# Attention over 32 sequences of mixed length: running counts in place of token waits, early zero rows, stores on two queues, a tiled first batch and branch hints

## The chip, the cores and the metric

The kernel runs on one core of a Trainium2 chip. The metric is the device time of one execution in microseconds (us). Three runs of the kernel before took 423.67, 424.69 and 424.82; their median is 424.69.

## The reference

There are 32 sequences of at most 512 rows, 8 heads of 64 columns, and a length for each sequence (64 to 511). Rows beyond a sequence's length are zero in the output.

```
output = np.zeros_like(x)                      # (32, 512, 512) float32
for b in range(batch):
    seq_len = lengths[b]
    qkv = np.matmul(x[b, :seq_len], w_qkv)     # w_qkv: (512, 1536)
    q, k, v = np.split(qkv, 3, axis=-1)        # then (8 heads, seq_len, 64)
    scores = scale * np.matmul(q, k.transpose(0, 2, 1))
    attn = np.exp(scores - scores_max)
    attn = attn / (np.sum(attn, axis=-1, keepdims=True) + 1e-08)
    output[b, :seq_len] = np.matmul(attn, v).transpose(1, 0, 2).reshape(seq_len, dim)
```

The lengths are known to the kernel only when it runs; the draw is the same each time.

## The kernel before

**Order of the batches.** On the chip the 32 lengths are sorted in falling order, and the batches are taken in 16 pairs. Each pair gets a class N, the longer length rounded up to a multiple of 32, and T, the number of 128-row tiles in N. For this draw the classes are 512 and 448 (T=4), 384, 352 three times, 320 and 288 (T=3), 256, 224 twice, 192 and 160 twice (T=2), and 128 and 96 (T=1). Classes 480 and 416 do not occur. Every engine's program holds one loop body per class that a pair can have, one behind the other (`loops`, L571): a compare and branch enters body k, a second one at its end goes back to its start, and the program falls through or jumps over a body whose class has no pair. At each body's start `next_class` (L562) loads the following pair's class from a table.

**A body.** It has two halves, h = 0 and 1. Half h does the attention of batch h of the pair: scores (tokens S of the order, into the PSUM buffers s0 and s1 in turn), their exp on ACT, then attention times values (A0 to A3, two heads each), which DVE normalizes by a reciprocal (L370), a mask (L376 or L385) and a multiplication (L396) into `onat`. In the same half stand the projections of the other batch of the sorted order, g = 1 − h: for T ≥ 3 Q and K of two heads each, for T=2 both in one group of two (B0 to B3), and values V0 to V3; these go to the PSUM banks a0 and a1 in turn and are emptied by DVE (L275, L308). `ORDER` (L420) is the order of these tokens, written out by hand for T=4, 3 and 2; T=1 has its own in `half` (L426).

**Waits.** Each instruction that needs another engine's result is preceded by `take` (L34): a wait until a semaphore has reached a number and an instruction that takes the number off again, line 37 in the profile. Only then does the engine go on.

**Queues.** SP issues the transposes of x into xT (L621, one for each 128 rows, from the float16 copy that POOL casts, L768), the loads of x (L629), and for each half two stores of 256 columns each (L675; for T=1 one store, L683). Each store waits for the half's normalization (`s_of`). The order in a half is: transposes, for T=3 a fill of zero rows (L594), store 0, load, store 1. For T=2 and T=1 ACT issues the fills of zero rows at the body's start.

**The first batch.** Lengths are sorted; meanwhile the weights arrive. x of the first batch comes as two loads of 512 KB (L638). DVE casts half of the query and key weights (L866) and then x (L870), ACT the other half (L715). TensorE transposes x in 16 steps (L519) into `pa`, ACT and DVE empty one bank each (L530, L532), and the projections of the first batch follow. POOL writes the start value 0.01 of the exp buffer `ep` (L761).

Of the kernel before, what the change touches and what calls it, by code (L numbers as in the profile page):

```python
# [21 lines left out]
class Prog:  # L22


    def __init__(self, busy, pair=None):
        self.ops = {"pe": [], "act": [], "dve": []}
        self.busy = dict(busy)
        self.pair = {"s0": pair, "s1": pair}
        self.signals = []
# [4 lines left out]
    def take(self, eng, sem, n=1):  # L34
        def fn(e):
            e.wait_ge(sem, n)
            e.nop().then_inc(sem, -n)  # L37

        self.ops[eng].append(fn)
# [35 lines left out]
def kernel(  # L75
# [32 lines left out]
    zt = sb("zt", [P, D], FP32)  # L108
    len_b = sb("len_b", [B, 2 * B], I32)
# [25 lines left out]
    pa16 = pa.bitcast(F16)  # L135
    pav = nc.alloc_psum_tensor("pav", [P, 2 * MAXS], FP32).ap()
# [9 lines left out]
    s_x0 = [sem("s_x00"), sem("s_x01")]  # L146
    s_c0 = [sem("s_c00"), sem("s_c01")]
# [3 lines left out]
    s_zero = sem("s_zero")  # L151
    s_zd = sem("s_zd")
# [3 lines left out]
    s_wr = {g: sem(f"s_wr{g}") for g in ("act", "dve", "v")}  # L156
# [16 lines left out]
    free = {b: sem(f"e_{b}") for b in banks}  # L173
# [7 lines left out]
    def group(pr, b, eng, mms, evac):  # L181
        if b in free:
            acquire(pr, b)
# [10 lines left out]
        pr.add("pe", pe)  # L194
        pr.take(eng, full[(b, eng)])
# [120 lines left out]
    def attnv(pr, h, i, T):  # L316
# [35 lines left out]
        else:  # L352
# [15 lines left out]
        group(  # L368
            pr, "av", "dve", mms,
            lambda e: e.reciprocal(out=rv, in_=den).then_inc(s_r, 1),  # L370
        )
        pr.take("dve", s_r)
        if h == 0 or T == 1:
            pr.add(
                "dve",
                lambda e: e.tensor_scalar(  # L376
                    out=last, in0=last, scalar1=3.0e38, scalar2=now[0][:, 1, T - 1 : T],
                    op0=ALU.min, op1=ALU.mult,
                ).then_inc(s_m, 1),
            )  # L380
        else:
            byt = flat.rearrange("p (t a) -> p t a", t=T)
            pr.add(
                "dve",
                lambda e: e.scalar_tensor_tensor(  # L385
                    out=byt, in0=byt, scalar=3.0e38,
                    in1=now[0][:, 1, 0:T].unsqueeze(2).broadcast_to(list(byt.shape)),
                    op0=ALU.min, op1=ALU.mult,
                ).then_inc(s_m, 1),
            )  # L390
        for j in (0, 1) if T == 1 else (i // 2,) if T != 4 or i % 2 == 0 else ():
            pr.take("dve", s_od[h][j], 16)
        pr.take("dve", s_m)

        def mult(e):
            ins = e.tensor_tensor(  # L396
                out=dst,
                in0=num,
                in1=rv.unsqueeze(len(sh) + 1).broadcast_to([P, *sh, HD]),
                op=ALU.mult,  # L400
            )
            if fin:
                ins.then_inc(s_of[h][i // 2], 1)

        pr.add("dve", mult)

    def acquire_carry(pr, mms):
# [16 lines left out]
    }  # L424

    def half(pr, h, T, N, st):  # L426
# [10 lines left out]
        if T == 1:  # L437
            start_proj()
            qk(pr, st["bank"], g, [(i, 0) for i in range(NPAIR)], N, P)
            qk(pr, st["bank"] ^ 1, g, [(i, 1) for i in range(NPAIR)], N, P)  # L440
            vproj(pr, st["bank"], g, 0, 1)
            pr.signals.append(s_xtf[g])
            pr.take("pe", s_on[h])
            attnv(pr, h, 0, 1)
            acquire(pr, f"a{st['bank'] ^ 1}")
            scores(pr, h, g, 0, 0, 1, N)
            st["bank"] ^= 1
# [3 lines left out]
        first = True  # L451
        for tok in ORDER[T].split():
            if tok == "S":
                i, k = units.pop(0)
                scores(pr, st["slot"], g if i == 0 else h, i, k, T, N)
                st["slot"] ^= 1
            elif tok[0] == "A":
# [3 lines left out]
                attnv(pr, h, int(tok[1]), T)  # L461
            else:
                start_proj()
                i = int(tok[1])
                if tok[0] == "V":
                    vproj(pr, st["bank"], g, i, T)
                elif tok[0] == "B":
                    qk(pr, st["bank"], g, [(i, 0), (i, 1)], N, 256)
                else:
                    qk(pr, st["bank"], g, [(i, "QK".index(tok[0]))], N, MAXS)  # L470
                st["bank"] ^= 1
        assert not units

    def make_body(N):
        T = -(-N // P)
        pr = Prog(CANON, 0)
        for g in ("pe", "act", "dve"):
            pr.add(g, lambda e: next_class(e))
        st = {"slot": 0, "bank": 0}
        for h in range(2):  # L480
            st["x"] = False
            pr.add("dve", lambda e: set_now(e))
            half(pr, h, T, N, st)
# [25 lines left out]
    def make_prologue():  # L509
        pr = Prog({})  # L510
        pr.add("pe", lambda e: e.wait_ge(s_id, 1))

        def tr(e):
            for j in range(2):
                e.wait_ge(s_c0[j], 1)
                for t in (2 * j, 2 * j + 1):
                    for c in range(NC):
                        o = pa16[:, c // 2, (c % 2) * MAXS + t * P : (c % 2) * MAXS + (t + 1) * P]
# [396 lines left out]
```

## Time and profile before

| what | us |
|---|---|
| median of three runs | 424.69 |
| the profiled execution | 426.59 |
| its span in the profile | 424.8 |
| start, up to the first projection | 17.9 |
| first batch's projections | 17.1 |
| bodies with T=4 (2 pairs) | 83.5 |
| bodies with T=3 (6 pairs) | 164.5 |
| bodies with T=2 (6 pairs) | 103.4 |
| bodies with T=1 (2 pairs) | 31.5 |
| last multiplication to the end | 6.9 |

The stages are stretches of the one profiled execution, from a first matmul to the next stage's first. PE is TensorE's matmuls, PEld its weight loads, DVE VectorE, ACT ScalarE, POOL GpSimd, SP the engine that issues most DMAs; a row with a "q" behind the engine (SPq, ACTq, PEq) is that engine's queue or sequencer. A timeline row gives start, length, engine, line, operation, output from input, the count of like instructions, and in brackets the idle time before it with what ended it. A row of the waits gives engine, tile and line, what was waited for, the sum in us, how often, and the longest.

### The profile page before, as it was taken

To read this page: it belongs to the slowest core of one execution; us is meant where nothing else is said; L and a number is where in the kernel's file an instruction comes from. 1 tells how busy PE (TensorE), PEld (TensorE's weight loads), DVE (VectorE), ACT (ScalarE), POOL (GpSimd) and SP (SyncE) were. 2 spreads that over 40 slices of the span, in tenths; PEclk is the share of its full clock that TensorE was granted. 3 is DMA by queue.
4 is the path that set the end of the run, shared out by engine and by line. 5 is a ranking of instruction groups with operands and counts; after the bars stand their busy time and mean duration, and the time that the engine had idled before them with its cause. 6 is when DMAs were issued, how large, how long until landed. Compare 5 with 4: busy or idle time off the path is not lost. (4 is left out here: it accounts for less than half of the span.)

```text
span 424.8 us, 13689 instructions
## 1 busy us (share of the span) xinstructions
PE 354.6 (83%) x4818; PEld 255.4 (60%) x4819; DVE 252.8 (60%) x539; ACT 208.4 (49%) x270; POOL 66.8 (16%) x91
## 2 busy tenths in 40 slices
PE   0589999799889999999999999998788888785741
PEld 0237666466546666666666666677677777674530
DVE  4546666366626666666666756667666676665331
ACT  3035778477636666665666645545334342331000
POOL 5912020202011011100111001111112111210100
PEclk9999999899969999999999999999999999999676
DMA  7854454446535545556455564694676757767471
GB/s 281 313 161 139 150 103 151 96 151 94 177 89 158 168 132 169 167 158 200 125 164 181 158 192 111 185 275 138 221 203 198 260 138 240 250 164 254 83 257 53
DMA packets 83019, 73.35 MB, mean 173 GB/s; under 512 B 42512, under 2 KB 62992, under 8 KB 82960
## 3 DMA queue, kind: packets, MB, share of 16 engines
q1 hardware_dynamic: 77472, 61.04, 50.0%
q10 hardware_dynamic: 5488, 11.54, 7.4%
q8 instruction: 35, 0.57, 0.6%
q14 instruction: 24, 0.20, 0.2%
HBM read 29.37 MB, written 33.55 MB: 148 GB/s over the span
## 5 line engine op out<-in xcount | busy, mean ns | idle before, releaser
L245 ACT ACTIVATE ep<-psc 128x704 f16<-128x704 f32 (+5 forms) x265 | 204.0, 820 | 195.0 <-ACTq L37 195.0
L203 PE MATMUL pa<-xT,w_r 128*128 128x352 f16 (+11 forms) x1056 | 166.7, 296 | 32.8 <-PEq L37 32.3
L275 DVE CAST qkT<-pa 128x352 f16<-128x352 f32 (+5 forms) x192 | 108.0, 563 | 96.5 <-DVEq L37 95.3
L203 PEld LDWEIGHTS pa<-xT,w_r 128*128 128x128 f16 x1056 | 84.4, 101 | 85.2 <-issue 67.1
L203 PE MATMUL pa<-w_r,xT 128*128 128x128 f16 (+1 forms) x1296 | 96.8, 223 | 1.6 <-PEq L37 1.1
L203 PEld LDWEIGHTS pa<-w_r,xT 128*128 128x128 f16 x1296 | 79.2, 98 | 16.7 <-issue 10.3
L203 PE MATMUL psc<-qkT 64*128 64x352 f16 (+11 forms) x656 | 71.6, 303 | 12.0 <-PEq L37 11.9
L308 DVE TENSOR_TENSOR v_aug<-pa,masks 128x384 f16<-128x384 f32 (+2 forms) x116 | 60.8, 524 | 27.1 <-DVEq L37 25.3
L203 PEld LDWEIGHTS pav<-v_aug,ep 128*128 128x128 f16 x1792 | 70.1, 98 | 10.3 <-issue 2.2
L203 PE MATMUL pav<-v_aug,ep 128*128 128x65 f16 x1792 | 74.8, 195 | 0.2 <-issue 0.2
L773 POOL CAST v_aug<-masks 128x24 f16 (+4 forms) x33 | 9.1, 274 | 334.9 <-POOLq L586 334.9
L396 DVE TENSOR_TENSOR onat<-pav,rcp 128x512 f32<-128x512 f32 (+1 forms) x68 | 53.4, 785 | 10.0
L203 PEld LDWEIGHTS psc<-qkT 64*128 64x128 f16 x656 | 25.9, 94 | 33.2 <-issue 22.9
L768 POOL CAST x<-x_nat 128x1536 f16<-128x1536 f32 (+3 forms) x34 | 43.9, 1291 | 5.2 <-POOLq L586 4.7
L370 DVE RECIPROCAL rcp<-pav 128x8 f32<-128x8 f32 (+1 forms) x68 | 14.4, 212 | 6.3 <-DVEq L37 5.7
L376 DVE TENSOR_SCALAR rcp<-rcp,masks 128x4 f32<-128x4 f32 (+2 forms) x36 | 8.3, 229 | 7.3 <-DVEq L37 7.3
L519 PE MATMUL pa<-ident,x 128*128 128x128 f16 x16 | 2.0, 308 | 9.7 <-DVE x L870 9.7
L385 DVE SCALAR_TENSOR_TENSOR rcp<-rcp,masks 128x8 f32<-128x8 f32 (+1 forms) x32 | 5.4, 168 | 6.4 <-DVEq L37 3.7
L519 PEld LDWEIGHTS pa<-ident,x 128*128 128x128 f16 x16 | 1.5, 139 | 10.1 <-issue 9.5
L761 POOL MEMSET ep<- 128x1024 f32 x6 | 7.1, 1224 | 0.0
L288 DVE TENSOR_SCALAR v_aug<-pa,masks 128x512 f16<-128x512 f32 x4 | 3.0, 753 | 4.2 <-DVEq L37 4.2
L530 ACT COPY xT<-pa 128x1024 f16<-128x1024 f16 x1 | 1.0, 1012 | 7.9 <-ACTq L37 7.9
(42 smaller groups left out, 21.8 us busy)
## 6 DMA issues: line engine op xcount, KB each, us to landing
out_dram<-onat SPq DMA_DIRECT2D x24, 384.0 KB, 2.6
x_nat<-in_x_dram SPq DMA_DIRECT2D x12, 768.0 KB, 4.8
x_nat<-in_x_dram SPq DMA_DIRECT2D x8, 1024.0 KB, 5.9
x_nat<-in_x_dram SPq DMA_DIRECT2D x14, 512.0 KB, 4.3
out_dram<-onat SPq DMA_DIRECT2D x28, 256.0 KB, 2.8
out_dram<-zt ACTq DMA_DIRECT2D x12, 512.0 KB, 3.6
out_dram<-onat SPq DMA_DIRECT2D x8, 512.0 KB, 3.5
out_dram<-zt SPq DMA_DIRECT2D x12, 256.0 KB, 2.0
```

Source lines behind the costliest of these rows:

```text
L203: return lambda e: e.matmul(o, lhsT, rhs, start=start, stop=stop)
L245: lambda e: e.activation(out=dst, in_=src, func=AF.Exp, scale=scale),
L275: group(pr, b, eng, mms, lambda e: e.tensor_copy(out=dst, in_=src))
L308: lambda e: e.tensor_tensor(out=v_aug[h][:, 0:T, 2 * i : 2 * i + 2, 0:HD], in0=pa[:, bank, 0 : T * P].rearrange("p (t a d) -> p t a d", a= ...
L370: lambda e: e.reciprocal(out=rv, in_=den).then_inc(s_r, 1),
L376: lambda e: e.tensor_scalar(out=last, in0=last, scalar1=3.0e38, scalar2=now[0][:, 1, T - 1 : T], op0=ALU.min, op1=ALU.mult,).then_inc(s_m, 1),
L385: lambda e: e.scalar_tensor_tensor(out=byt, in0=byt, scalar=3.0e38, in1=now[0][:, 1, 0:T].unsqueeze(2).broadcast_to(list(byt.shape)), op0= ...
L396: ins = e.tensor_tensor(out=dst, in0=num, in1=rv.unsqueeze(len(sh) + 1).broadcast_to([P, *sh, HD]), op=ALU.mult,)
L519: ins = e.transpose(o, x16[0][:, t, c * P : (c + 1) * P], ident)
L761: e.memset(ep32[:, i, a], 0.01)
L768: e.tensor_copy(out=x16[h][:, 0:T, :], in_=x_nat[h][:, 0:T, :]).then_inc(s_xc[h], 1)
L773: e.tensor_copy(out=v_aug[h][:, 0:T, :, HD], in_=src[:, 0, 0:T].unsqueeze(2).broadcast_to([P, T, NH]),).then_inc(s_on[h], 1)
```

## The change

**Waits.** `take` puts a running count into the instruction that needs it: the n-th taking in a body waits for the total so far, and only the last one in a body takes the total off.

```diff
     def take(self, eng, sem, n=1):
+        key = (eng, sem.name)
+        total = self.count[key] = self.count.get(key, 0) + n
+        here = self.final[key] = len(self.ops[eng])
+
         def fn(e):
-            e.wait_ge(sem, n)
-            e.nop().then_inc(sem, -n)
+            e.wait_ge(sem, total)
+            if self.final[key] == here:
+                e.nop().then_inc(sem, -total)
```

**Orders.** O and P are a half's stores 0 and 1, issued by ACT (`act_store`); R, M and X are reciprocal, mask and multiplication as tokens of their own; b1 is a B1 that ACT empties in place of DVE.

```diff
     ORDER = {
-        4: "S S Q0 A0 S S K0 V0 S S Q1 A1 S S K1 V1 S S Q2 A2 S S K2 V2 S S Q3 A3 S S K3 V3",
-        3: "S S Q0 A0 K0 S S V0 Q1 A1 S S K1 V1 S S Q2 A2 K2 S S V2 Q3 A3 S S K3 V3",
-        2: "S S B0 V0 B1 A0 V1 A1 S S B2 V2 B3 A2 V3 A3",
+        4: "S S Q0 A0 S S K0 V0 S S Q1 A1 S S K1 V1 S S Q2 A2 S S K2 V2 S S Q3 A3 S S K3 V3 O",
+        3: "S S Q0 A0 K0 S S V0 Q1 A1 S S K1 V1 S S Q2 A2 K2 S S V2 Q3 A3 S S K3 V3 O",
+        2: "S B0 S V0 A0 b1 A1 R1 M1 X1 V1 S S B2 V2 A2 A3 O V3 P B3",
     }
```

**Hints.** The class of the next pair is read within half 0, behind its third projection, and TensorE then also gets a hint on whether the body of the class behind the next will be passed over.

```diff
+    def read_class(pr, h, N):
+        if h == 0:
+            for g in ("pe", "act", "dve"):
+                pr.add(g, lambda e: next_class(e))
+            k = CLASSES.index(N)
+            if k + 2 < len(CLASSES):
+                def hint(e):
+                    cur, far = regs[e.engine][1], regs["far"]
+                    e.reg_alu(far, cur, k + 2, ALU.is_lt)
+                    ahead[k + 1] = e.mark_branch_hint_location(far)
+                pr.add("pe", hint)
...
-            e.br_cmp(cur, k, lab, out_, "IS_EQ")
+            br = e.br_cmp(cur, k, lab, out_, "IS_EQ")
+            if name == "pe" and k in ahead:
+                br.branch_hint(ahead[k])
```

The two places in the first half of the body for class 224 (T=2) where TensorE's instructions move are these. `psc` is the scores' PSUM buffer, `pa` the projections', `pav` that of attention times values; `e_a0`, `e_a1` and `e_s1` say that a buffer has been emptied, `s_xt1` that xT of the other batch is there. Before, behind the two groups of scores:

```order
L203 MATMUL pa<-xT,w_r 128x224 [waits s_xt1,e_a0]
L203 MATMUL pa<-xT,w_r 128x224 x7
L203 MATMUL pa<-w_r,xT 128x128 [waits e_a1]
L203 MATMUL pa<-w_r,xT 128x128 x7
L203 MATMUL pa<-xT,w_r 128x224 [waits e_a0]
L203 MATMUL pa<-xT,w_r 128x224 x7
L203 MATMUL pav<-v_aug,ep 128x65 [waits s_on0]
L203 MATMUL pav<-v_aug,ep 128x65 x7
```

Three projections follow one another. With the change, behind the first group of scores:

```order
L220 MATMUL pa<-xT,w_r 128x224 [waits s_xt1,e_a0]
L220 MATMUL pa<-xT,w_r 128x224 x7
L220 MATMUL psc<-qkT 128x224 [waits e_s1]
L220 MATMUL psc<-qkT 128x224 x3
L220 MATMUL pa<-w_r,xT 128x128 [waits e_a1]
L220 MATMUL pa<-w_r,xT 128x128 x7
L220 MATMUL pav<-v_aug,ep 128x65 [waits s_on0]
L220 MATMUL pav<-v_aug,ep 128x65 x7
L220 MATMUL pa<-xT,w_r 128x224 [waits e_a0]
L220 MATMUL pa<-xT,w_r 128x224 x7
L650 ISA
L651 TENSOR_LOAD cls
```

The second group of scores now stands between the first two projections and the first attention group ahead of the third, behind which the class is read.

**Zero rows.** In the first eight pairs (ranks below 16; all with T=4 and 3) SP writes, at the body's start and for both halves, rows 128 to 511 of the mirrored batch of the sorted order (rank 31 − r), and for T=3 the last tile of its own. ACT waits once, at rank 16, for all these rows to have landed. The fills of T=2 and T=1 are gone.

```diff
+                e.br_lt(rank, B // 2, lab, out_)
...
+                for h in range(2):
+                    e.reg_add(mir, rank, h)
+                    e.reg_sub(mir, B - 1, mir)
+                    zero_fill(e, batch_of(e, mir, tmp, 0), 1, s_zm)
+                    if T < NT:
+                        zero_fill(e, batch_of(e, rank, tmp, h), T, s_zd)
...
                 for h in range(2):
                     wait_dec(e, s_xtf[h])
                     to_xT(h, N)
-                    elif T == 3:
-                        zero_fill(e, batch_of(e, rank, tmp, 0), T)
...
+                    wait_dec(e, s_xc[1 - h])
+                    load(1 - h, 5, T)
+                    if T > 1 and "P" not in ORDER[T]:
+                        wait_dec(e, s_of[h][1])
+                        store(e, batch_of(e, rank, tmp, 0), h, 1, T)
```

On SP's queue the body of class 352 (T=3) begins before with its transposes, a fill of one tile and a store (`s_xtf0`: xT may be overwritten; `s_of00`: store 0's columns are ready):

```order
L621 DMA_TRANSPOSE xT<-x_0 128x4x128 [waits s_xtf0]
L621 DMA_TRANSPOSE xT<-x_0 128x4x128
L621 DMA_TRANSPOSE xT<-x_0 128x4x96
L589 ISA
L590 TENSOR_LOAD idx
L591 ISA
L594 DMA out_dram<-zt 128x512
L589 ISA [waits s_of00]
L590 TENSOR_LOAD idx
L591 ISA
L675 DMA out_dram<-onat 128x3x256
```

With the change it begins with two pairs of fills, of which this is the second, ahead of the same transposes:

```order
L693 DMA out_dram<-zt 128x3x512
L680 ISA
L681 TENSOR_LOAD idx
L682 ISA
L693 DMA out_dram<-zt 128x512
L768 UNCONDITIONAL_BRANCH
L721 DMA_TRANSPOSE xT<-x_0 128x4x128 [waits s_xtf0]
L721 DMA_TRANSPOSE xT<-x_0 128x4x128
L721 DMA_TRANSPOSE xT<-x_0 128x4x96
L680 ISA [waits s_xc1]
```

The fills moved from behind the transposes to ahead of them and became four; store 0 is no longer on this queue, so that the wait behind the transposes is the one for the cast of x (`s_xc1`).

For T=1 the second half's rows on SP before are these:

```order
L621 DMA_TRANSPOSE xT<-x_1 128x4x128 [waits s_xtf1]
L589 ISA [waits s_of10]
L590 TENSOR_LOAD idx
L591 ISA
L683 DMA out_dram<-onat 256x1x256
L589 ISA [waits s_xc0]
L590 TENSOR_LOAD idx
L591 ISA
L629 DMA x_nat<-in_x_dram 128x512
```

And with the change (class 96):

```order
L721 DMA_TRANSPOSE xT<-x_1 128x4x96 [waits s_xtf1]
L680 ISA [waits s_xc0]
L681 TENSOR_LOAD idx
L682 ISA
L729 DMA x_nat<-in_x_dram 128x512
```

The store with its wait for the normalization has left SP; ACT issues it behind the half's exp.

**The first batch.** x comes as four loads of 256 KB, the value weights' load waits for the first of them, ACT casts all query and key weights, and DVE casts x a tile at a time; TensorE transposes each tile into a PSUM place of its own, and ACT and DVE empty them in turn. ACT fills `ep` between its first exps. TensorE runs 26 matmuls on zeros ahead of that.

```diff
+            e.wait_ge(s_zero, 1)
+            warm(8)
             e.wait_ge(s_hot, 1)
...
             ins.then_inc(full[("av", "dve")], 1)
+            warm(18)
...
-            for j in range(2):
-                e.wait_ge(s_c0[j], 1)
-                for t in (2 * j, 2 * j + 1):
...
+            for t in range(NT):
+                e.wait_ge(s_c0[t], 1)
+                for c in range(NC):
+                    ins = e.transpose(
+                        home[t][:, c * P : (c + 1) * P], x16[0][:, t, c * P : (c + 1) * P], ident
+                    )
+                ins.then_inc(s_t0[t], 1)
...
-            for c in (0, 2):
+            for c in range(NC):
                 e.wait_ge(s_wqk[c], 16)
                 ins = e.copy(out=w_r[:, c, 0 : 2 * D], in_=w_f[:, c, 0 : 2 * D])
```

At the very end ACT's loop sets a semaphore that SP waits for (`s_fin`), then SP waits for all stores.

More of the change, by code (lines that the diff above doesn't have):

```diff
@@ L367, in attnv @@
         num, den = res[..., 0:HD], res[..., HD]
[L368 to L405, printed above, removed]
+        close(pr, "av", "dve", mms)
```

271 lines of the change are left out of this document (173 added, 98 removed).

## The prediction

> **What bounds the kernel now.** I read the page's totals first, then the busy time by stage, since the loop bodies differ by class.
>
> ```profile
> span 424.8 us, 13689 instructions
> PE 354.6 (83%) x4818; PEld 255.4 (60%) x4819; DVE 252.8 (60%) x539; ACT 208.4 (49%) x270; POOL 66.8 (16%) x91
> ```
>
> TensorE is busy in 83% of the span, and no other engine comes near. So what counts is the 70 us in which it has nothing to do, and the time in which it runs slowly. The table by stage shows where these lie. Its columns are the stretch and its length, then busy time (and instructions) of PE, PEld, DVE, ACT and POOL, the granted clock, the DMA share and GB/s. The first six rows are start of data, prologue, and bodies with T=4, T=3, T=2 and T=1; the last two are pieces at half clock.
>
> ```profile
> 0.00:17.90 17.90, 2.29 (x18) 1.68 (x19) 10.21 (x23) 4.40 (x5) 12.82 (x24) 1.00 0.81 300
> 17.90:35.00 17.10, 15.79 (x106) 7.50 (x106) 7.50 (x11) 4.09 (x4) 5.17 (x4) 1.00 0.66 209
> 35.00:118.50 83.50, 77.18 (x1026) 50.02 (x1024) 49.89 (x98) 58.62 (x64) 8.84 (x8) 0.98 0.49 127
> 118.50:283.00 164.50, 158.35 (x2129) 109.15 (x2130) 104.16 (x216) 98.61 (x144) 21.70 (x26) 0.98 0.53 160
> 283.00:386.40 103.40, 83.39 (x1338) 73.62 (x1335) 68.98 (x168) 38.82 (x49) 14.94 (x23) 1.00 0.69 202
> 386.40:417.90 31.50, 17.62 (x208) 13.44 (x208) 12.05 (x24) 3.86 (x5) 3.32 (x8) 0.78 0.62 190
> 76.90:80.40 3.50, 3.13 (x23) 1.66 (x24) 0.43 (x1) 1.73 (x2) 1.77 (x2) 0.51 0.20 42
> 117.90:124.70 6.80, 6.12 (x44) 3.38 (x45) 1.11 (x2) 2.58 (x4) 1.75 (x2) 0.50 0.31 66
> ```
>
> T=4 and T=3 are 92% and 96% busy: little is to be had there. T=2 loses 20.0 us of 103.4, T=1 13.9 of 31.5, and 17.9 us go by before the first projection.
>
> **Startup: first batch tile by tile.** The DMA-queue rows are issues; the line after them says how long such loads took to land.
>
> ```profile
> 6.20 1.02 SPq L638 DMA_DIRECT2D x_nat<-in_x_dram  x2
> DMA to landing us min/median/max: 4.3/4.9/5.6
> 12.55 2.95 DVE L870 CAST x<-x_nat 128x1024 f16<-128x1024 f32 x2
> 16.74 0.69 DVE L532 COPY xT<-pa 128x1024 f16<-128x1024 f16 x1 [1.24 <-DVEq L37]
> 17.95 3.57 PE L203 MATMUL pa<-xT,w_r 128*128 128x512 f16 x8 [1.37 <-PEq L37]
> 26.52 1.90 PE L203 MATMUL pa<-xT,w_r 128*128 128x512 f16 x8
> 31.07 3.99 PE L203 MATMUL pa<-w_r,xT 128*128 128x128 f16 x64 [0.17 <-issue]
> 21.01 5.23 SPq L621 DMA_TRANSPOSE xT<-x  x4
> ```
>
> DVE comes to x at 12.55, behind its weight casts (L866), and ends at 15.5; the last half of x had landed by 6.8 + 5.6 = 12.4. The diff moves those weight casts to ACT, and the value load no longer competes with x, so I put the last tile at 11.8. From there: cast 2.95 / 4 = 0.74, four transposes about 0.4, evacuation 0.69 / 2 = 0.35, and three handoffs of 0.15 give a first projection near 13.8, 4.2 earlier. The first eight matmuls took 3.57 (0.45 each), the later eight 1.90 (0.24): TensorE began slow. If the 26 warm matmuls hold it fast, four pairs of groups at 2.15 (1.90 and a handoff), about 0.8 of first wait and V at 3.99 take 13.4 instead of the 17.1 of the second stage; body start is 27.2, a gain of 7.8. I take half of the slow time as still there: **−6.5**, between −3.5 (slow as before, x 0.6 late) and −8. What hides the rest: ACT's ep fills, six of about 1.0 like its four exps there (4.09), lie between those, beside the projections. The second batch's transposes are on the queue till 26.24 even if nothing speeds them; some 1.2 later they have landed, at 27.4, and their first reader comes behind two groups of scores, at 28.4. If that cover is gone, each microsecond of it costs one.
>
> The Trainium skill, "TensorE: Matmul & The Clock Gate", Part 4, says that transposes do not count as busy for the clock gate, so a warm-up ahead of 16 transposes may be lost. The slow eight at 17.95 followed transposes, which agrees, though they had no warm-up before. By it this term would be −4.1 instead of −6.5.
>
> **Branch hints.** The two rows are the first scores of the bodies behind a class that is left out (480, 416).
>
> ```profile
> 77.27 0.93 PE L203 MATMUL psc<-qkT 64*128 64x448 f16 x4 [2.94 <-PEq L37]
> 118.58 0.82 PE L203 MATMUL psc<-qkT 64*128 64x384 f16 x4 [3.38 <-PEq L37]
> ```
>
> TensorE's sequencer was late there by 2.94 and 3.38 us, and the half-clock pieces above follow at once. At half clock, busy time of 3.13 and 6.12 is about half lost: 1.56 + 3.06 = 4.6. Idle and slowness are 10.9. No first scores behind another jump waited longer than 0.9 (the row of T=2, below), so the skipped body is what these two share, and the hint is given for exactly that skip. I leave 0.5 a place: **−10**. The ends are 0 (the hint does nothing) and −10.9.
>
> **Token waits, T=4 and T=3.** A wait that was an instruction of its own becomes part of the instruction behind it.
>
> ```profile
> PE pa L203 <- PEq L37: 5.1, 18, 0.5
> PE psc L203 <- PEq L37: 3.4, 1, 3.4
> ```
>
> The first is T=3: 18 waits of 0.28 on projection banks; the second is the skip again. No row parts the token's share of the 0.28 from the wait for the bank; I take 0.17, most of it, since an evacuation starts and ends sooner by tokens as well: 18 × 0.17 = **−3** for T=3, between 0 and −5.1. For T=4 **0**: no row there waits besides the skip.
>
> **Zero rows early.** SP issues four fills (two of 768 KB and two of a tile) ahead of the T=3 body's first transposes; two in T=4.
>
> ```profile
> out_dram<-zt ACTq DMA_DIRECT2D x4, 768.0 KB, 4.6
> 151.87 3.84 SPq L621 DMA_TRANSPOSE xT<-x  x3
> DMA to landing us min/median/max: 2.4/2.5/2.6
> 163.39 0.76 PE L203 MATMUL pa<-xT,w_r 128*128 128x352 f16 x4 [0.18 <-PEq L37]
> 386.20 1.38 ACTq L594 DMA_DIRECT2D out_dram<-zt  x2
> ```
>
> The three transposes are on the queue till 155.7; the last lands near 156.9, and its reader starts at 163.39: 6.5 us of cover. An issue of a fill is 1.38 / 2 = 0.69, with its index load 0.9: four put the transposes 3.5 later. Their 2 MB at the 300 GB/s of the first stage need 6.8, so up to 3.3 more is still moving then. 3.5 + 3.3 = 6.8 against 6.5: **0**, with 1.5 us for each of six bodies (+9) as the bad end, where the loads in flight share the rate. What is queued behind them: transposes, the next x load and the j=1 store, in this order. T=4 has the same cover with half the fills. The fills that disappear from T=2 ease its DMA; I count nothing for it.
>
> **T=2, new order.** Waits of TensorE in that stage, and one of them:
>
> ```profile
> PE pa L203 <- PEq L37: 14.5, 24, 0.8
> PE psc L203 <- PEq L37: 4.6, 6, 0.9
> 302.82 0.93 PE L203 MATMUL pa<-xT,w_r 128*128 128x224 f16 x8 [0.47 <-PEq L37]
> ```
>
> B1 at 302.82 waits until DVE has emptied B0's bank: three projections run back to back on two banks. That is 14.5 + 4.6 = 19.1 us in twelve halves, 1.6 each. The new order puts scores or attention between them, has ACT empty one B (DVE is 68.98 busy of 103.4, ACT only 38.82), and delays the normalizing. Laid out by hand for 224 columns, a wait of about 0.4 stays at the first B, behind the previous half's late evacuation, and 0.25 at V2; one more change of operand 0.1. So 0.85 to 0.9 a half is gone, with the shorter handoffs of two more groups hidden: 12 × 0.9 = **−11**, between −6 (half as good) and −15. ACT's cover: an evacuation of about 0.6 beside its exps, 38.82 + 12 × 0.6 = 46 of some 92. The j=0 and j=1 stores behind exps on ACT hold up exps by one issue each; scores have two slots, so I count nothing, and 0.5 a half (6 us) if that cover is gone, in the −6.
>
> **T=1, stores on ACT's queue.**
>
> ```profile
> 389.06 2.01 SPq L621 DMA_TRANSPOSE xT<-x  x1
> DMA to landing us min/median/max: 6.2/6.2/6.2
> 395.37 3.57 PE L203 MATMUL pa<-xT,w_r 128*128 128x128 f16 x32 [5.18 <-PEq L37]
> 401.42 1.53 PE L203 MATMUL pa<-xT,w_r 128*128 128x96 f16 x32
> 405.28 0.34 PE L203 MATMUL psc<-qkT 64*128 64x96 f16 x8
> 406.83 0.69 DVE L396 TENSOR_TENSOR onat<-pav,rcp 128x512 f32<-128x512 f32 x1
> 407.78 1.21 SPq L621 DMA_TRANSPOSE xT<-x  x1
> 410.64 2.72 PE L203 MATMUL pa<-xT,w_r 128*128 128x96 f16 x32 [5.02 <-PEq L37]
> 417.15 0.69 DVE L396 TENSOR_TENSOR onat<-pav,rcp 128x512 f32<-128x512 f32 x1
> 418.51 0.59 SPq L683 DMA_DIRECT2D out_dram<-onat  x1
> ```
>
> Projections wait 5.2 and 5.0 us for transposes, and then run at half the speed (3.57 against 1.53 for nearly the same). The first transposes were issued at 389.06, behind the two zero fills of 386.20 and took 6.2 to land, against 2.5 elsewhere; those fills are gone here. The second were issued at 407.78, since SP first stores a half's result, which waits for the half's last multiplication, and loads. With the stores on ACT, SP goes on once x is cast. The half at 401.42 is the model: to 405.62 it takes 4.2. Three such from 386.5, and 401.42 to 407.52 (6.1) for the last, end at 405.2 instead of 417.84: **−12.6**, between −4 (one wait stays) and −14. Late next: the load, cast and transposes of a batch, which have two halves, 8.4 us.
>
> **End.** From 417.84 the store, a pointless last load and its landing take 6.9. The store goes at once from ACT, the load is earlier: about 5, **−1.8** (0 to −3).
>
> **Sum.** −6.5 −10 −3 −11 −12.6 −1.8 = −44.9: span 379.9. The profiled execution took 426.59, 1.8 around its span, so 381.7 by it; it is 1.9 above the median of the runs shown, 424.69, from which the same sum gives 379.8. I say 380.
>
> **The rivals.**
> - The hint does nothing: the two gaps and their slow pieces stay, 380 + 10 = 390. For it: nothing in the trace shows a hint. Against: the gaps are only at skips. 0.12.
> - Zero rows delay T=3 transposes: 380 + 9 = 389. For it: 6.8 against 6.5. Against: T=3 moves 160 GB/s where the start moved 300. 0.13.
> - Two queues are no two transfers: the waits at 395.37 and 410.64 stay, being bound by data, and only the issue and its index load leave SP, 4 × 0.6 = 2.4 (by 418.51) of the 12.6: 380 + 10 = 390. For it: the 6.2 at 389.06 was data, not issue. Against: what it shared the queues with leaves, and at 410.64 the issue was late, 2.9 ahead of its reader. 0.10. The Trainium skill, "DMA: Bandwidth & Descriptors", section "Issuing engines are not separate DMA queues", has it so: a second engine saves only the sequencer's time. It does not speak of an engine that waits for results before it issues.
> - Warm-up is lost on the transposes: projections at 17.1 instead of 13.4, so 7.8 − 3.7 = 4.1 for 6.5: 382.4. 0.06, next to the forecast.
> - Everything better: T=2 at −15, hints −10.9, start −8, T=1 −14, T=3 −5: 371. 0.06.
> - Slower than before: the hint makes TensorE's sequencer fetch the wrong way at the body boundaries that now go without a gap. A miss costs (10.9 / 2) 5.4; there are 15 boundaries, two missed already. From 44.9 / 5.4 = 8.3, that is 9 of the other 13, the time is above 424.7; all 13 give 380 + 13 × 5.4 = 450. For it: the hint's register also depends on classes that come later, which no row shows. Against: it is set for one skip alone. 0.03.
>
> **How the numbers follow.** The forecast has 0.50, its own range 373 to 388. Every rival but the last lies at 371 to 390, and two of them together near 400. Bad ends of T=2 (5) and of the start (3) may add to one of the +10 rivals: 390 + 8 = 398. So 369 to 398 leaves out little more than the last rival and pairs of bad ends. About 0.3% is what a measurement of this kernel can tell from no change. Faster 0.96, same 0.01, slower 0.03.
>
> **What would show it.** The gaps at the first scores for 448 and 384, and the granted clock behind them; projection waits in T=2, 19.1 us now, at about 8; starts of T=1 projections 4.2 apart; body start near 28, and its first eight projections at 1.9 rather than 3.6; T=3 transposes landing ahead of the half's first projection. The forecast is wrong if TensorE keeps either skip gap, if a T=3 half waits over 1 us for xT, or if T=2's DVE, now near 69 of fewer us, sets the pace.

## The result and the profile after

The changed kernel takes 379.88 us (median of four runs, 378.38 to 382.25) against 424.75 for the kernel before (median of four, the three runs above and one more). The ratio is 0.8939, with a 95% interval of 0.8872 to 0.9006. The profiled execution took 378.38, with a span of 376.5. It is the fastest of its four, while the profiled execution of before was above its median: so the two spans differ by 48.3 us and the medians by 44.9. Here and below, medians and ratios leave out runs more than 1.5% above the fastest of their kernel, and a ratio is of mean times.

The page's totals of the changed kernel:

```profile
span 376.5 us, 12671 instructions
PE 347.0 (92%) x4844; PEld 242.5 (64%) x4845; DVE 244.2 (65%) x529; ACT 221.6 (59%) x291; POOL 58.1 (15%) x85
```

TensorE's busy time fell by 7.6 us only, its idle time from 70 to 29.5. To see where, both kernels are cut at the same events: the first scores of a body of the first class, of 384, of 256, of 128, the last multiplication, and the end. First the busy time by stage of the kernel before (columns as in the prediction; T=4, T=3, T=2, T=1, end), then that of the changed kernel, with its two starting stages ahead.

```profile
34.99:118.58 83.59, 77.19 (x1026) 50.06 (x1025) 49.90 (x98) 58.62 (x64) 8.84 (x8) 0.98 0.49 127
118.58:281.54 162.96, 156.89 (x2114) 108.00 (x2114) 103.26 (x215) 98.61 (x144) 21.09 (x24) 0.98 0.53 158
281.54:385.05 103.51, 84.45 (x1346) 74.51 (x1345) 69.01 (x169) 37.99 (x48) 15.54 (x24) 1.00 0.70 205
385.05:417.84 32.79, 18.03 (x216) 13.66 (x216) 12.90 (x26) 4.69 (x5) 3.32 (x8) 0.79 0.62 189
417.84:424.80 6.96, 0.00 (x0) 0.00 (x0) 0.00 (x0) 0.00 (x0) 0.00 (x0) 0.53 0.27 77
```

```profile
0.00:13.39 13.39, 8.79 (x45) 3.79 (x47) 6.38 (x25) 6.66 (x8) 3.36 (x17) 1.00 0.79 281
13.39:26.76 13.37, 12.49 (x104) 6.79 (x105) 7.60 (x11) 9.43 (x10) 5.95 (x4) 1.00 0.72 215
26.76:104.03 77.27, 75.50 (x1028) 46.97 (x1026) 49.81 (x97) 58.62 (x64) 8.84 (x8) 1.00 0.73 194
104.03:261.94 157.91, 151.46 (x2114) 104.64 (x2112) 103.53 (x215) 98.62 (x144) 21.04 (x24) 1.00 0.82 229
261.94:353.25 91.31, 85.10 (x1346) 70.15 (x1345) 64.47 (x159) 43.56 (x61) 15.59 (x24) 1.00 0.64 173
353.25:371.69 18.44, 13.64 (x216) 10.21 (x216) 12.41 (x24) 4.69 (x5) 3.33 (x8) 1.00 0.51 142
371.69:376.50 4.81, 0.00 (x0) 0.00 (x0) 0.00 (x1) 0.00 (x0) 0.00 (x0) 0.64 0.16 56
```

The lengths in the second column subtract: start 34.99 − 26.76 = 8.2, T=4 6.3, T=3 5.1, T=2 12.2, T=1 14.4, end 2.2 us less. The granted clock is 1.00 in every stage in which TensorE works, and T=3 moves 229 GB/s instead of 158, since the zero rows are written there.

The rows of TensorE's timeline that answer to those of the prediction (first projections, first scores of the first body and its first projection, the two bodies behind a skipped class, two projections of T=1):

```profile
13.39 1.89 PE L220 MATMUL pa<-xT,w_r 128*128 128x512 f16 x8 [0.83 <-PEq L45]
26.76 0.61 PE L220 MATMUL psc<-qkT 64*128 64x512 f16 x4
29.14 1.02 PE L220 MATMUL pa<-xT,w_r 128*128 128x512 f16 x4 [1.77 <-PEq L45]
67.59 0.55 PE L220 MATMUL psc<-qkT 64*128 64x448 f16 x4
104.03 0.50 PE L220 MATMUL psc<-qkT 64*128 64x384 f16 x4
357.71 1.95 PE L220 MATMUL pa<-xT,w_r 128*128 128x128 f16 x32 [0.15 <-PEq L45]
361.35 1.52 PE L220 MATMUL pa<-xT,w_r 128*128 128x96 f16 x32
```

The eight first projections run at full speed, the two skips have no wait at all, and projections of T=1 no longer wait 5 us. New is a wait of 1.77 us at 29.14, for the transposes of the second batch. TensorE's waits of the changed kernel in T=3 (the first row; two more there sum to 0.6) and in T=2 (three rows, the last one ahead of the first body with T=1):

```profile
PE pa L220 <- PEq L45: 5.1, 3, 2.3
PE pa L220 <- DVE v_aug L325: 4.1, 12, 0.7
PE pa L220 <- DVE qkT L292: 0.3, 1, 0.3
PE psc L220 <- PEq L45: 1.4, 1, 1.4
```

T=3 waits 5.1 us as before, but they are three waits of up to 2.3 instead of 18 of 0.28. T=2 waits 5.8 instead of 19.1, of which 4.4 ahead of projections instead of 14.5.

### The profile page after: what moved, and what is told of

Its sections match the earlier page's. It is cut to its first block, busy times and chain, and to the rows that moved or that the text cites. A ratio compares the mean times of both kernels' runs of the same rounds, so it can differ in the third digit from the quotient of the medians.

```text
span 376.5 us, 12671 instructions
## 1 busy us (share of the span) xinstructions
PE 347.0 (92%) x4844; PEld 242.5 (64%) x4845; DVE 244.2 (65%) x529; ACT 221.6 (59%) x291; POOL 58.1 (15%) x85
## 5 line engine op out<-in xcount | busy, mean ns | idle before, releaser
L220 PE MATMUL pa<-xT,w_r 128*128 128x352 f16 (+11 forms) x1056 | 159.2, 286 | 13.2 <-PEq L45 8.2
L292 DVE CAST qkT<-pa 128x352 f16<-128x352 f32 (+5 forms) x180 | 101.2, 563 | 62.0 <-PE pa L220 59.9
L220 PEld LDWEIGHTS pa<-xT,w_r 128*128 128x128 f16 x1056 | 80.7, 98 | 64.6 <-issue 30.1
L220 PEld LDWEIGHTS pav<-v_aug,ep 128*128 128x128 f16 x1792 | 67.2, 98 | 9.5 <-issue 0.6
L220 PE MATMUL pav<-v_aug,ep 128*128 128x65 f16 x1792 | 71.7, 194 | 0.1
L220 PEld LDWEIGHTS psc<-qkT 64*128 64x128 f16 x656 | 20.6, 94 | 23.0 <-issue 12.5
L389 DVE RECIPROCAL rcp<-pav 128x8 f32<-128x8 f32 (+1 forms) x68 | 14.6, 215 | 15.6 <-PE pav L220 12.4
L900 PE MATMUL psc<-zt 128*128 128x512 f16 x26 | 7.3, 441 | 1.7 <-DVE zt L922 1.7
L290 ACT CAST qkT<-pa 128x448 f16<-128x448 f32 (+3 forms) x12 | 6.0, 499 | 3.3 <-ACTq L45 2.6
L631 ACT ACTIVATE ep<-tiny 128x1024 f32<-128x1024 f32 x6 | 6.0, 1051 | 0.0
L807 ACT CAST w_r<-w_f 128x1024 f16<-128x1024 f32 x4 | 4.2, 1046 | 1.2 <-DMA w_f<-in_w_qkv_dram 1.2
```

The costliest lines, as they stand in the source:

```text
L220: return lambda e: e.matmul(o, lhsT, rhs, start=start, stop=stop)
L290: group(pr, b, eng, mms, lambda e: e.copy(out=dst, in_=src))
L292: group(pr, b, eng, mms, lambda e: e.tensor_copy(out=dst, in_=src))
L389: pr.add("dve", lambda e: e.reciprocal(out=rv, in_=den).then_inc(s_r, 1))
L631: lambda e, i=i, a=a: e.activation(out=ep32[:, i + 1, a], func=AF.Copy, in_=tiny.unsqueeze(2).broadcast_to([P, NT, MAXS // 2]),).then_inc( ...
L900: e.matmul(psc[:, 1, 0, :], zt16[:, 0:P], zt16[:, 0:MAXS], start=True, stop=True)
```

## The experiments

Each kernel is timed beside runs of the kernel before on the same chip; ratios are to that kernel. Stages are read from each one's profile and cut as above. The start alone differs between profiles of the same prologue, from 26.8 to 31.4 us, so stages are compared rather than spans.

**Hints away from the changed kernel.**

```diff
-                    ahead[k + 1] = e.mark_branch_hint_location(far)
```

> The changed kernel without the branch hint; the class is still read behind the third projection. Theory (the hint removes the gaps): the first scores for 448 and for 384 wait about 2.9 and 3.4 us again and stretches at half clock follow; the time is about 10 us above the changed kernel's 380, so near 390, a ratio to the kernel before of 0.915 to 0.92. Rival (reading the class half a body earlier is what removed them): no gap over 0.5 us at either place, the time within 2 us of 380, a ratio near 0.894.

388.57 us, ratio 0.9126 (0.9064 to 0.9188). The first scores of the two bodies on its timeline:

```profile
73.49 0.56 PE L220 MATMUL psc<-qkT 64*128 64x448 f16 x4 [2.83 <-issue]
114.21 0.50 PE L220 MATMUL psc<-qkT 64*128 64x384 f16 x4 [2.66 <-issue]
```

Both waits are back, with a half-clock stretch of 3.4 us behind each, and the median is 8.7 us above the changed kernel's. In the trace TensorE's branch instructions at the two places take 3.97 and 3.77 us, in the kernel before 3.38 and 3.79, and in the changed kernel none takes over 0.38. The hint removes the gaps; the earlier class read doesn't.

**Hints alone on the kernel before**, set at the body's start behind `next_class`.

```diff
         for g in ("pe", "act", "dve"):
             pr.add(g, lambda e: next_class(e))
+        k = CLASSES.index(N)
+        if k + 2 < len(CLASSES):
...
+            pr.add("pe", hint)
```

> The kernel before with the hint alone, set at a body's start behind the class load. Theory: both gaps go and the granted clock stays at 1.00 to the bodies with T=1; about 10 us less than the kernel before's 425, so near 415, a ratio of 0.973 to 0.98. Rival (the hint only helps with the other parts, or costs misses elsewhere): a ratio of 0.995 or above, or gaps of 2 us and more at other bodies' first scores.

424.67 us, ratio 1.0001 (0.9962 to 1.0039): nothing. Its timeline at the same two places:

```profile
73.15 0.55 PE L203 MATMUL psc<-qkT 64*128 64x448 f16 x4 [0.23 <-PEq L37]
113.79 0.58 PE L203 MATMUL psc<-qkT 64*128 64x384 f16 x4 [3.52 <-PEq L37]
```

The first gap is gone, the second is not; the two branches take 0.47 and 3.77 us. T=4 takes 80.23 instead of 83.59, but T=2 105.94 instead of 103.51, where six first scores wait 5.6 us instead of 4.6 and one projection 1.6. The hint's instructions stand between one body's last matmul and the next one's first, which may be why the first scores wait longer; that is not shown. So the hint did not pay at every place: behind the third projection it worked for both skips. Whether the distance to the jump decides that, was not tried.

**Fills behind half 0's load** in place of ahead of its transposes.

```diff
-                e.br_lt(rank, B // 2, lab, out_)
...
                 for h in range(2):
...
                     load(1 - h, 5, T)
+                    if h == 0:
...
+                        e.br_lt(rank, B // 2, lab, out_)
...
```

> The changed kernel with the four early fills of zero rows behind the half 0 load of x instead of ahead of half 0's transposes; as many bytes. The changed kernel's trace has three waits for xT in T=3 halves, 0.8, 2.3 and 2.0 us, 5.1 in all. Theory (the fills' issue and data ahead of the transposes cause them): none of these over 0.5 us, T=3 from 157.9 to about 153 us, the time about 5 us below the changed kernel. Rival (the bytes themselves, wherever they stand on the queue, keep the transposes late): the waits stay or move to the following half 0, and the time is the changed kernel's within 1 us.

374.98 us, ratio 0.8826 (0.8762 to 0.8889), 4.9 below the changed kernel. T=3 and its only wait in the profile:

```profile
105.94:257.65 151.71, 150.96 (x2115) 104.59 (x2114) 103.70 (x215) 98.61 (x144) 20.95 (x24) 1.00 0.82 234
PE pa L220 <- DVE qkT L292: 0.2, 1, 0.2
```

T=3 is 6.2 us shorter, with the same bytes in all, and TensorE is busy for 150.96 of 151.71. So the fills' place ahead of the transposes cost 6.2 us, not their data.

**The second batch's x ahead of the value weights.**

```diff
             e.wait_ge(s_x0[0], 16)
+            load(1, 1, NT)
             e.dma_start(
                 out=w_f[:, :, 2 * D : 3 * D],
...
-            load(1, 1, NT)
...
+            cast(1, NT)
             e.wait_ge(s_wv, 16)
...
-            cast(1, NT)
```

> The changed kernel with the second batch's x loaded and cast ahead of the value weights. The changed kernel waits 1.77 us for the second batch's transposes at its first body's first projection. Theory (the value weights ahead of x on the queue and on POOL cause it): that wait is gone, the time 1.8 us lower, and the value projections don't wait. Rival (the value weights become late instead): a wait of 1 to 3 us ahead of the value projections, the time within 1 us of the changed kernel or above it.

380.08 us, ratio 0.8943 (0.8860 to 0.9027): no gain. The wait of 1.77 is not in its profile, but that proves little: its first scores come at 30.26 us, since TensorE ran at half clock from 14.8 to 21.6, and the kernel with the fills moved, with the old order of loads, is as late (30.21) and has no such wait either. With a slow prologue the transposes are early enough anyway. The last kernel of this section has x first and a fast start: there the transposes, ahead of all fills in both kernels, leave SP at 24.60 instead of 27.78, and the body's first projection runs at 28.52 with no wait, ahead of the 29.14 of the changed kernel. So the order of loads can remove the wait; that it gains time is not shown.

**T=2 in its order of before.**

```diff
-        2: "S B0 S V0 A0 b1 A1 R1 M1 X1 V1 S S B2 V2 A2 A3 O V3 P B3",
+        2: "S S B0 V0 B1 A0 V1 A1 S S B2 V2 B3 A2 V3 A3 O",
```

> The changed kernel with the order of T=2 of the kernel before (DVE empties every projection; store 0 on ACT at the half's end, store 1 on SP as for T=3). T=2 took 103.5 us before and 91.3 with the change. Theory (the order is what gained): T=2 takes 100 to 103 us, with 24 waits of about 0.5 us on projection banks, and the time is 9 to 11 us above the changed kernel. Rival (running counts shorten the handoffs that were those waits): T=2 takes 94 to 97 us, and the time is 3 to 5 us above.

385.71 us, ratio 0.9104 (0.9033 to 0.9175), 5.8 above the changed kernel, though T=1 is 1.7 longer here too. T=2 took 96.16, as the rival has it: 4.9 more than the changed kernel, and 7.4 less than the kernel before, which has the same order but also its fills in this stage. The stage, and TensorE's waits in it:

```profile
262.80:359.00 96.20, 85.14 (x1348) 73.89 (x1348) 69.55 (x169) 38.01 (x49) 15.54 (x24) 1.00 0.56 159
PE pa L220 <- DVE qkT L292: 6.1, 16, 0.9
PE pa L220 <- PEq L45: 3.7, 9, 0.8
```

**B1 emptied by DVE** in the new T=2 order.

```diff
-        2: "S B0 S V0 A0 b1 A1 R1 M1 X1 V1 S S B2 V2 A2 A3 O V3 P B3",
+        2: "S B0 S V0 A0 B1 A1 R1 M1 X1 V1 S S B2 V2 A2 A3 O V3 P B3",
```

> The changed kernel with its new T=2 order, but DVE empties the B1 group, not ACT. Theory (the bank is freed in time because it does not queue behind DVE's work): waits of about 0.5 us at one or two places of each half, T=2 at 96 to 99 us. Rival (the order alone, with projections no longer back to back, is enough): T=2 at 91 to 93 us.

384.28 us, ratio 0.9066 (0.9018 to 0.9114). T=2 took 94.5, between the two ranges expected. Its waits for DVE rise from 4.1 in 12 to 6.3 in 17 places, and DVE is busy for 70.66 of the stage instead of 64.47:

```profile
261.90:356.40 94.50, 85.80 (x1348) 69.99 (x1348) 70.66 (x171) 38.10 (x48) 15.54 (x24) 1.00 0.62 167
PE pa L220 <- DVE v_aug L325: 6.3, 17, 0.7
```

ACT's evacuation is worth 3.2 of the 4.9 that the order gains.

**Token waits in the changed kernel.**

```diff
-            e.wait_ge(sem, total)
-            if self.final[key] == here:
-                e.nop().then_inc(sem, -total)
+            e.wait_ge(sem, n)
+            e.nop().then_inc(sem, -n)
```

> The changed kernel with token waits as before (a wait and an instruction that takes the number off, at each taking). Theory of the prediction (a token costs about 0.17 us of each short wait on a projection bank): T=3 gains 3 us, T=2 some 12 x 0.2 = 2.4, the start and T=1 another 1; the time 6 us above the changed kernel. Rival A (what T=3 gained, 7 us beside its waits for xT, is tokens, and T=2's handoffs likewise): 10 to 15 us above. Rival B (the waits are hidden once the order has slack): within 2 us.

402.68 us, ratio 0.9451 (0.9380 to 0.9522): 23 us above the changed kernel, beyond every bound stated. T=3 and T=2 of this kernel, and TensorE's waits ahead of projections in each (in T=3 those for the transposes are among them):

```profile
110.05:275.55 165.50, 155.22 (x2113) 107.19 (x2114) 103.59 (x215) 98.61 (x144) 21.09 (x24) 0.99 0.77 217
275.55:377.09 101.54, 86.74 (x1347) 70.23 (x1347) 64.69 (x159) 43.75 (x61) 15.53 (x24) 1.00 0.56 156
```

```profile
PE pa L219 <- PEq L44: 9.3, 18, 2.1
PE pa L219 <- PEq L44: 11.4, 23, 0.8
```

T=3 is 7.6 longer, T=2 10.2, T=4 3.5 and T=1 0.5; the start is 2.6 later, as in most profiles. Not all of it is the tokens' own for certain. T=3 has a half-clock stretch of 3.4 us behind a wait of 2.08, which costs 1.7 of the 7.6. T=4 has two single waits of 2.1 and 1.0 and another such stretch, against the changed kernel's one wait of 1.77, and these explain 3.1 of its 3.5. In T=2 the clock stays at 1.00. So some 17 us of the 23 are the price of tokens in the profile, and whether the rest comes with them is open. The order of T=2 with tokens gains 2.0 over the kernel before (103.51 to 101.54), counts with the old order 7.4, both together 12.2; the kernel without fills, below, takes 1.6 off the first two.

**T=1 stores on SP again.**

```diff
-            act_store(pr, h, 0, T)
...
                     to_xT(h, N)
+                    if T == 1:
+                        wait_dec(e, s_of[h][0])
+                        bi = batch_of(e, rank, tmp, 0)
+                        e.dma_start(
...
+                            in_=onat[h][:, :, 0, :],
+                        ).then_inc(s_od[h][0], 16)
```

> The changed kernel with the T=1 stores back on SP, between the transposes and the next load. T=1 from its first scores to the last multiplication took 32.8 us before and 18.4 with the change. Theory (SP's wait for the normalization holds back load and transposes): T=1 takes 24 to 27 us, with waits of 2 to 5 us for transposes at two or more projections, the time 6 to 9 us above the changed kernel. Rival (the rule that a second queue saves issue time alone; the rest was the zero fills' data): T=1 takes 20 to 21 us, 4 x 0.6 = 2.4 more than the changed kernel.

385.94 us, ratio 0.9071 (0.9010 to 0.9133). Its T=1 stage, its end, and one projection of T=1:

```profile
357.10:378.26 21.16, 14.91 (x216) 10.76 (x216) 12.10 (x24) 4.70 (x5) 3.31 (x8) 0.92 0.35 102
378.26:385.20 6.94, 0.00 (x0) 0.00 (x0) 0.00 (x0) 0.00 (x0) 0.00 (x0) 0.64 0.37 104
368.60 1.59 PE L220 MATMUL pa<-xT,w_r 128*128 128x96 f16 x32 [3.34 <-PEq L45]
```

The time is 6.1 above the changed kernel, as the theory has it, but the stage is not: T=1 is 2.7 longer, near the 2.4 of the rival, and the end 2.1 longer, as before the change. The start and T=3 of this profile are longer too, with a half-clock stretch in each. The Trainium skill, "DMA: Bandwidth & Descriptors", section "Issuing engines are not separate DMA queues", allows a second engine the sequencer's time alone; the 2.7 agree in size, but one wait of 3.34 for transposes is in this kernel and not in the changed one, so a wait on SP is saved, not only issue.

**The kernel before without its fills of T=2 and T=1.**

```diff
-                        zero_fill(e, batch_of(e, rank, tmp, h), T)
+                        e.nop().then_inc(s_zd, 16)
```

> The kernel before without the fills of zero rows of T=2 and T=1; those rows of the output are not written. Theory (the first T=1 wait of 5.18 us was data of the two fills of 386.20, the second of 5.02 was SP's order): the transposes behind the first T=1 half land in 2.5 to 3.5 us instead of 6.2, that wait falls to about 2, the second stays near 5; T=1 at 27 to 30 us, T=2 unchanged within 1 us. Rival (both waits are SP's order): both stay at 5, T=1 at 32 to 33.

This kernel leaves those rows of the output unwritten. 415.66 us, ratio 0.9773 (0.9715 to 0.9832). The stages T=2 and T=1, the two projections of T=1 that waited 5 us, and the landing of the transposes of 389.88:

```profile
280.92:382.82 101.90, 84.51 (x1346) 74.51 (x1345) 69.11 (x169) 37.99 (x48) 15.54 (x24) 1.00 0.54 146
382.83:406.71 23.88, 15.01 (x216) 11.52 (x216) 13.00 (x26) 4.69 (x5) 3.31 (x8) 0.93 0.44 115
389.88 1.95 PE L203 MATMUL pa<-xT,w_r 128*128 128x128 f16 x32 [1.96 <-PEq L37]
395.62 2.72 PE L203 MATMUL pa<-xT,w_r 128*128 128x96 f16 x32 [2.10 <-PEq L37]
DMA to landing us min/median/max: 3.5/3.5/3.5
```

T=1 is 8.9 us shorter with SP's order untouched: the fills alone. Both waits fell, from 5.2 and 5.0 to about 2, 6.1 together, and TensorE's busy time from 18.03 to 15.01, with less half clock. So the second wait is no matter of SP's order alone, for which both theories took it. T=2, expected unchanged within 1 us, is 1.6 shorter: waits on projection banks stay (15.6 against 14.5), but those of the first scores fall from 4.6 to 1.5.

**No warm matmuls.**

```diff
-            e.wait_ge(s_zero, 1)
-            warm(8)
...
-            warm(18)
```

> The changed kernel without the 26 matmuls on zeros. Theory (they warm the clock, and it stays so over the 16 transposes): the first eight projections take 3.6 us instead of 1.9, and projections are slow for some 4 to 8 us; the body's first scores 3 to 4 us later. As the first body then waited 1.77 us for transposes of the second batch, 1.8 of this is hidden: the time 1.5 to 2.5 us above the changed kernel. Rival (the transposes end the warm state or make it by themselves): first scores within 0.5 us of the changed kernel.

379.34 us, ratio 0.8934 (0.8888 to 0.8981): the changed kernel's time. Its first projections take 3.57 us and the body begins at 31.35, so 4.6 later than in the changed kernel's profile. The profile gives the clock as 1.00 from 14.12 to 18.57, as the second row of the prediction's table does for the kernel before, yet these matmuls take nearly twice the 1.90 of later ones; neither trace holds a clock record ahead of 23 us, so there the matmuls' lengths decide. Yet the medians agree; the next two experiments bear on it.

**Fills late and x first.**

```diff
+                    if h == 0:
...
+                        e.br_lt(rank, B // 2, lab, out_)
...
+            load(1, 1, NT)
...
+            cast(1, NT)
```

> The changed kernel with the fills behind half 0's load and the second batch's x ahead of the value weights. If the two waits have the causes given, 5.1 + 1.8 = 6.9 us go, near 373 and a ratio to the kernel before of about 0.878. If one of them only moves, 375 to 378.

375.17 us, ratio 0.8823 (0.8783 to 0.8863): what the fills give alone. First projections and the body's first scores, with all 26 warm matmuls:

```profile
14.36 3.57 PE L220 MATMUL pa<-xT,w_r 128*128 128x512 f16 x8 [0.83 <-PEq L45]
31.18 0.60 PE L220 MATMUL psc<-qkT 64*128 64x512 f16 x4
```

They are as slow as without. The trace records half clock from 12.3 to 22.5 us here. Of the eight other profiles with 26 warm matmuls, the changed kernel's among them, the body begins at 26.8 and 27.1 in two, and at 29.3 to 31.4 in six, each of these with a half-clock stretch there.

**The same, and matmuls on zeros up to the first projection.**

```diff
-            warm(18)
+            warm(25)
...
                 ins.then_inc(s_t0[t], 1)
+                for _ in range(2 if t < NT - 1 else 3):
+                    e.matmul(psc[:, 1, 0, :], zt16[:, 0:P], zt16[:, 0:MAXS], start=True, stop=True)
```

> The kernel with late fills and the second batch's x first, and besides with matmuls on zeros that go on up to the first projection: 25 in place of 18 ahead of the transposes, two behind each of the first three tiles' transposes and three behind the last. In most profiles so far the granted clock fell to half between 12 and 15 us, in the pause of real matmuls around the transposes, and the body's first scores stood at 29.5 to 31.4 us; in two it stayed at 1.00 and they stood at 26.8 and 27.1. Theory (transposes with pauses don't hold the clock, matmuls do): no half-clock stretch ahead of the body, its first scores at 26.5 to 27.5, and 3 to 4 us less than the kernel without them, 375.2: near 372, a ratio of 0.873 to 0.876. Rival (the fall comes whatever runs there): first scores at 30 to 31, 375 us as without them.

375.43 us, ratio 0.8810 (0.8774 to 0.8846). The same two rows, and the body's first projection:

```profile
14.61 1.89 PE L220 MATMUL pa<-xT,w_r 128*128 128x512 f16 x8 [0.18 <-PEq L45]
27.99 0.61 PE L220 MATMUL psc<-qkT 64*128 64x512 f16 x4
28.52 1.04 PE L220 MATMUL pa<-xT,w_r 128*128 128x512 f16 x4
```

The clock holds and the body begins 3.2 us earlier. But the time is the same: in this profile T=4 is 1.3 longer than in the kernel without these matmuls, T=3 0.7, T=2 1.0 and T=1 1.6, of which the last has a half-clock stretch of its own. What pays the 3.2 back in the other five runs is not known.

## Why the prediction was right, point by point

The time, 379.9, is the 380 of the forecast, and no term had the wrong sign. But several sizes and causes behind it were wrong, and misses of opposite sign cancel, so that coming within 0.1 us is luck. One of the prediction's own signs of being wrong came true: two T=3 halves wait over 1 us for xT (2.3 and 2.0).

- **Start, −6.5.** In the profiled run the body start moved by 8.2, and the new wait of 1.77 that the cover was to prevent takes it to 6.5. The transposes of the second batch left SP 1.5 later than in the trace of before (27.78 against 26.24), not earlier. In seven of nine profiles of this prologue TensorE is slow after the transposes, and the body start moved by 3.6 to 5.7: the rival "warm-up is lost", at 4.1, is the usual state, and the forecast's value, half of the slow time, was a mean of two cases that both occur. Without warm matmuls the time is the same.
- **Hints, −10.** Both gaps of 2.94 and 3.38 and the slow stretches went. Taking the hint away costs 8.7 us by the medians. That the hint removes them is shown; that it does so from any place is refuted. The branch instructions themselves were slow, by somewhat more than the gaps.
- **Token waits, T=4 0 and T=3 −3.** This is the term that was mis-sized. Tokens cost 7.6 in T=3 of the changed kernel (5.9 without the half clock), and 10.2 in T=2, for which the sum had no term of its own. T=3 of the kernel before, less the 3.1 that its half clock costs, against that of the kernel with the fills moved gives 8.2. The 0 for T=4 stands: the changed kernel has 75.5 there beside its 1.77 wait, the kernel before 75.7 beside gaps and clock. The step that failed is reading a token's price from the 18 waits of TensorE alone. TensorE's busy time is longer with tokens too: 156.89 in T=3 before, of which half clock explains 3.1, against 150.96 when nothing waits. A token may also delay every evacuation and exp; no run undoes them engine by engine, so that part is argued and not shown.
- **Zero rows, 0.** The rival "zero rows delay T=3 transposes" came true at 6.2 of its 9 us: three waits of 5.1, and some more in small pieces. The rows of class 320 in the changed kernel, of SP's queue, the landing of its transposes, and of their reader, then the waits of classes 352 and 288:

```profile
212.57 4.08 SPq L693 DMA_DIRECT2D out_dram<-zt  x4
216.78 4.81 SPq L721 DMA_TRANSPOSE xT<-x  x3
DMA to landing us min/median/max: 3.0/4.0/4.7
224.53 0.70 PE L220 MATMUL pa<-xT,w_r 128*128 128x320 f16 x4 [2.30 <-PEq L45]
145.42 0.76 PE L220 MATMUL pa<-xT,w_r 128*128 128x352 f16 x4 [0.80 <-PEq L45]
250.67 0.65 PE L220 MATMUL pa<-xT,w_r 128*128 128x288 f16 x4 [1.98 <-PEq L45]
```

The fills hold SP for 4.2 from 212.57 to 216.78, and then the transposes take 4.0 to land instead of 2.5. The forecast had 3.5 and up to 3.3 more against 6.5 of cover, and that cover was read from one half of class 352 and taken for all; the class 384 has no such wait, 352 one of 0.8, 320 and 288 have 2.3 and 2.0. The step that failed is the 0 for a sum with no margin. It hid in T=3's total: 162.96 − 157.91 = 5.1, of which the clock is 3.1; the other 2.0 are a gain of 8.2 less the 6.2 for the fills, and so look like the −3. The waits can cost more than their length: in five of the eight profiles with the fills ahead, half clock for 3.4 us sets in within 1.3 us of the end of one of 1.9 to 2.3, which costs 1.7 more; the changed kernel's profile has none.
- **T=2, −11.** Measured −12.2, but the order, for which the −11 stood, is worth 4.9 of it. If the parts add, 1.6 is the fills' leaving, for which the forecast counted nothing, and 5.7 the counts (101.90 to 96.16). Of the 14.5 us of waits on banks, counts with the old order leave 9.8 and the new order 4.4. ACT's evacuation carries 3.2 of the 4.9.
- **T=1, −12.6.** Measured −14.4, for another reason than the one that led. The sentence on the 6.2 us landing was the right one: the zero fills' leaving gives 8.9, SP's freedom from the stores 2.7. The remaining 2.8 are not parted. The rival that gave the two queues 2.4 us was right about them, and wrong about the time, as it left the fills out of account.
- **End, −1.8.** Measured −2.2, and it is the store on ACT: with the store on SP the end takes 6.94.

The Trainium skill, "TensorE: Matmul & The Clock Gate", Part 4, has it that transposes do not engage the full clock. Seven of nine profiles agree: the eight first projections take 2.73 to 3.57 us in spite of the warm matmuls, and 1.89 when matmuls stand between the transposes. In the other two, the changed kernel's own among them, the clock held without that; why, no run here shows. The pauses around the transposes are a rival that no run parts from the transposes, since the added matmuls fill both.

The best version of these is the changed kernel with its fills behind half 0's load: 374.98 against 379.88 us.

## What to carry to other kernels

A wait that needs an instruction of its own cost far more here than the waits of the busiest engine showed, so undo it alone to learn its price. Writes that nobody waits for can be moved to a stage with spare transfers, but behind the transfers that are waited for, not ahead of them. And terms that sum to the right time can each be wrong: undo parts one at a time, and read them by stage.

## What was not expected of the hardware

- A hint that is issued at a body's start removed one 3 us gap and not the other (0.23 and 3.52 us), while behind the third projection it removed both.
- 26 matmuls ending at 9.1 to 10.4 us did not reliably keep the clock up to a first projection at 14; nine more among the transposes and seven ahead of them did, in the one profile taken.
- Half clock came in stretches of 3.4 us, or two or three times that, except at a kernel's end, and a wait of 2 us could bring one on.
- Without the zero fills at the bodies' starts, the transposes of one tile landed in 3.5 us instead of 6.2, and T=1 took 23.9 instead of 32.8.
